# A hybrid encoder block's w_down products: where the fourth weight sum is made, and a place of its own for some raw weight blocks

## The chip, the cores and the metric

The kernel runs on one core of one Trainium2 chip. The metric is the time of one execution on the device in microseconds (us); the profile's page gives the span from the first to the last instruction of one execution. The engines are TensorE (PE: matmul; PEld: its weight loads), VectorE (DVE), ScalarE (ACT), GpSimd (POOL) and SyncE (SP), on which nearly all the transfers (DMA) of this kernel are issued. Each engine carries out its own instructions in order and waits for others through semaphores. SBUF is the on-chip memory in which tiles lie, PSUM the one that TensorE writes.

## The reference

One layer of an encoder on x of 1024 positions by 1024 channels, all in fp32:

```
h = RMSNorm(x)*(1+scale1)+shift1
[qA|kA|vA|qB|kB|vB|gA|gB] = h @ w_in
A: dilated sliding-window attention;  B: 2-D neighbourhood attention
m = sigmoid(gA)*(oA @ w_branch_dil) + sigmoid(gB)*(oB @ w_branch_na);  x += gate1 * (m @ w_out)
h2 = RMSNorm(x)*(1+scale2)+shift2;  u = depthwise_conv3(h2 @ w_up)
x += gate2 * ((gelu(u_g)*u_v) @ w_down)
y = RMSNorm_final(x)
```

The last product but the norm is the one that matters here: the GELU product a has 2816 channels (22 blocks of 128, called k-tiles), and w_down is 2816 by 1024.

## The kernel before, in words

**fp32 out of parts.** Each fp32 operand is split in two: a rounded copy, "hi", made by ScalarE, and the remainder, "lo" (source minus hi), made by GpSimd or VectorE (`split`, lines 57 and 61). A product takes three matmuls: hi·hi (line 1305), hi·lo (1306) and lo·hi (1307).

**Seven products for eight.** The large products are made in 2 × 2 blocks by a scheme of the Strassen-Winograd kind, with seven block products in place of eight. The weight blocks a11, a12, a21, a22 give seven left operands, in the order `11, S2, S1, S3, 12, S4, 22`, with

S1 = a21 + a22, S2 = S1 − a11, S3 = a11 − a21, S4 = a12 − S2.

`a_operands` makes them as a generator in four steps that the caller spreads over the products of the job before. It gets two raw blocks: raw[0] holds a11 and a12, raw[1] holds a21 and a22. GpSimd makes S1, S2 (both into one tile `ws` of the pool `big`) and S3 (in place of a21; lines 1255 to 1257). Then come the pairs: `whi`/`wlo` of raw[0], `wsh`/`wsl` of S2 and S1, `wsh`/`wsl` of S3 and a22. The fourth sum, S4, is VectorE's (line 1272), into a12's place in raw[0]; its hi and lo go into one more tile of `big`. So GpSimd has ten operations a job: three sums and seven remainders (128 × 384 each).

**The jobs of w_down.** Twelve jobs, numbered 0 to 11 (three groups of three pairs of k-tiles, times four pairs of row blocks q = 0 to 3), each of 7 × 3 × 3 = 63 matmuls of 128 × 512. While job n is multiplied, job n+1's weights are loaded (`down_load`, line 1419: two loads of 128 × 2 × 384, into two buffers `wraw`) and prepared. The pools set the rest: `whi`, `wlo`, `wsh`, `wsl` have two buffers or two and one, `big` nine, and PSUM six banks `pj`. `b_operands` loads and splits the right operands of the next group: six loads of 512 KB (line 1368), six GpSimd sums (1379, 1380) and splits (1359 to 1361). Results are put together by VectorE (1313 to 1330) and added to x (1411).

**What sets the order.** A list scheduler orders each engine's instructions after a simulated timeline. Two stretches are in the order of the code: SyncE's during jobs 0 to 2, and ScalarE's from the last w_up tile to job 2. A pool's buffer is used again when its last reader is done; the instruction that writes it waits for that.

**Names.** `pj` is a PSUM bank, `op` and `xb` are right operands, `x2` rows of x read back, `as` the GELU products in the chip's memory, `wc` a VectorE scratch tile. The number behind a name in the order is that of the instance.

Of the kernel before, what the change touches and what calls it, by code (L numbers as in the profile page):

```python
# [10 lines left out]
FT = mybir.dt.float32  # L11
FR = mybir.dt.float32r
AF = mybir.ActivationFunctionType
OP = mybir.AluOpType
# [5 lines left out]
KT = 8  # L20
# [4 lines left out]
G = 3  # L25
# [4 lines left out]
def hybrid_encoder(tc, xT, c, w_ada, small, w_in, p1_bias, p23_bias, na_bias, ln2_mult, ident, w_br, w_out,  # L30
                   w_up, w_down, out):
    nc = tc.nc
    act, dve, pool, pe, sp = nc.scalar, nc.vector, nc.gpsimd, nc.tensor, nc.sync

    const = tc.alloc_tile_pool(name="const", bufs=1)
    wpool = tc.alloc_tile_pool(name="w", bufs=2)
# [18 lines left out]
    def split(raw, hi, lo, lo_eng):  # L55

        act.activation(hi, raw, AF.Copy)  # L57
        n, cols = raw.shape[1], math.prod(raw.shape[1:])
        step = n // 2 if lo_eng is pool and cols > 512 and n % 2 == 0 else n
        for i in range(0, n, step):  # L60
            lo_eng.tensor_tensor(lo[:, i:i + step], raw[:, i:i + step], f(hi)[:, i:i + step], OP.subtract)  # L61
# [59 lines left out]
    work = tc.alloc_tile_pool(name="start", bufs=2, side="right", reuse_waits="tile")  # L121
# [150 lines left out]
    def v_wide(*sts):  # L272
        ps = [ps_s.tile([128, 512], FT, name="pv", bufs=3) if len(sts) == 1 else ps_g.tile([128, 512], FT, name="pj")
              for _ in sts]
        for k in range(KT):
            whi, wlo = (t[:, :, k] for t in v_all)
            for st, p in zip(sts, ps):
                hhi, hlo = (t[:, st % 4 * 128:st % 4 * 128 + 128] for t in h[st // 4, k])
                pe.matmul(p, hhi, whi, start=k == 0, stop=False)
                pe.matmul(p, hhi, wlo, start=False, stop=False)  # L280
                pe.matmul(p, hlo, whi, start=False, stop=k == KT - 1)
        return ps
# [136 lines left out]
    with tc.manual_schedule(engines={e.engine for e in (sp, act, dve, pool, pe)}):  # L419
# [37 lines left out]
        r = wpool.tile([128, KT], FT, name="rs", bufs=2)[:, :4]  # L457
# [18 lines left out]
        for q in range(4):  # L476
# [14 lines left out]
            last = 6 if q else 5  # L491
# [86 lines left out]
        for n, step in enumerate(v_steps[:9]):  # L578
# [14 lines left out]
            else:  # L593
                p = v_wide(*step[1:])
# [494 lines left out]
    for s in range(100):  # L1089
        n = 4 if s < 64 else 8 if s < 72 else 6 if s < 88 else 4  # L1090
# [24 lines left out]
    work = tc.alloc_tile_pool(name="gate", bufs=1, reuse_waits="tile")  # L1115
    o.append([work.tile([128, 4, S], FR, name=f"o1{n}") for n in ("hi", "lo")])
    g2 = g_scr.rearrange("(b m) p s -> m p b s", b=2)
    gates, ws, w_raw = {}, {}, {}
# [80 lines left out]
    for i in range(2 * KT):  # L1199
        m, hf = divmod(i, 2)  # L1200
# [16 lines left out]
        p = []  # L1217
# [22 lines left out]
    STEPS = (("11", "B11"), ("S2", "T2"), ("S1", "T1"), ("S3", "T3"), ("12", "B21"), ("S4", "B22"), ("22", "T4"))  # L1240
    names = tuple(b for _, b in STEPS)

    def a_operands(raw, n, work, st, lo_eng=pool, last=False, w_at=0, spot=None):


        spot = spot or big
        a11, a12, a21, a22 = raw[0][:, 0], raw[0][:, 1], raw[1][:, 0], raw[1][:, 1]
        ws = spot([128, 2, n, 128])
        S2, S1 = ws[:, 0], ws[:, 1]

        def pair(src, names, hi, lo, eng=pool):
            split(src, hi, lo, eng)
            for i, name in enumerate(names):
                st[name] = (hi[:, i], lo[:, i])
        pool.tensor_tensor(S1, a21, a22, OP.add)
        pool.tensor_tensor(S2, S1, a11, OP.subtract)
        pool.tensor_tensor(a21, a11, a21, OP.subtract)

        def outer(at):
            if w_at == at:  # L1260
                hi, lo = (wpool.tile([128, KT, 128], FR, name=t).rearrange("p (a b) m -> p a b m", a=2)[:, :, :n]
                          for t in ("whi", "wlo"))
                pair(raw[0], ("11", "12"), hi, lo, lo_eng)

        def s_tiles():
            pools = [work(t) for t in ("wsh", "wsl")]
            return [p.tile([128, 2, 4, 128], FR, name=t, bufs=b)[:, :, :n] for (p, b), t in zip(pools, ("wsh", "wsl"))]
        outer(0)
        yield
        pair(ws, ("S2", "S1"), *s_tiles())  # L1270
        if w_at != 3:
            dve.tensor_tensor(a12, a12, S2, OP.subtract)
        yield
        pair(raw[1], ("S3", "22"), *s_tiles())
        yield
        outer(3)
        if w_at == 3:
            dve.tensor_tensor(a12, a12, S2, OP.subtract)
        if last:
            p, b = work("wsl")  # L1280
            s4 = p.tile([128, 2, 4, 128], FR, name="wsl", bufs=b)[:, :, :n]
        else:
            s4 = spot([128, 2, n, 128], FR)
        pair(raw[0][:, 1:2], ("S4",), s4[:, 0:1], s4[:, 1:2])
        yield

    def products(st, n, moving, done, seq=range(7), in_psum=False, hold=None, spare=None):
# [46 lines left out]
    def reserve(tile_pool, tags):  # L1334
        for name, size, bufs in tags:
            tile_pool.tile([128, size // 4], FT, name=name, bufs=bufs)
# [7 lines left out]
    def big(shape, dtype=FT):  # L1344
        return keep.tile(shape, dtype, name="big", bufs=9)
# [63 lines left out]
    def acc(m, hf, src):  # L1409
        xx = x3[m, hf]  # L1410
        dve.scalar_tensor_tensor(xx, src, ada[:, 40 + m:41 + m], xx, OP.mult, OP.add)

    jobs = [(g0, q) for g0 in range(0, 9, G) for q in range(4)]

    def down_load(g0, q):
        raw = []
        for i in range(2):
            r = wpool.tile([128, KT, 128], FT, name="wraw").rearrange("p (a b) m -> p a b m", a=2)[:, :, :G]
            sp.dma_start(r, w_down[q + 4 * i].rearrange("p (a b) m -> p a b m", a=2)[:, :, g0:g0 + G])
            raw.append(r)  # L1420
        return raw
# [40 lines left out]
    def up_load(t):  # L1462
        raw = []
        for i in range(2):
            r = big([128, KT, 128]) if t in (0,) or t > 1 and t % 2 else wpool.tile([128, KT, 128], FT, name="wraw")
            sp.dma_start(r, w_up[t + FF * i])
            raw.append(r.rearrange("p (a b) m -> p a b m", a=2))
        return raw

    raw = [big([128, 2, 512]) for _ in range(4)]  # L1470
# [24 lines left out]
    raw = {0: up_load(0)}  # L1495
# [27 lines left out]

    work = tc.alloc_tile_pool(name="up", bufs=2, reuse_waits="tile")
    up2.append(work)
    tail, act_order, down_sts = [], contextlib.ExitStack(), [{} for _ in jobs]

    def extra(shape, dtype=FT):
# [53 lines left out]

    raw[1] = up_load(1)
    prep.append(a_operands(raw.pop(1), 4, s_home, sts[1], dve, spot=extra))
    next(prep[1])
    next(prep[1])
# [92 lines left out]
    nxt = a_operands(raw.pop(2), 4, s_home, sts[2], w_at=None, spot=extra)  # L1679
# [7 lines left out]
    for t in range(2, FF):  # L1687
        nxt = iter(())
        if t + 2 < FF:
            raw[t + 2] = up_load(t + 2)  # L1690
        if 0 < t < FF - 1:
            nxt = a_operands(raw.pop(t + 1), 4, s_home, sts[t + 1], last=t + 2 == FF)
            next(nxt)
        if t == FF - 1:
            act_order.enter_context(tc.manual_schedule(engines={act.engine}))
            next(first)
        for c, j in enumerate(gens[t] if t < 3 else up_products(t, sts[t])):
            if j in (1, 2, 5):
                next(nxt, None)
            if t == FF - 2 and j == 2:  # L1700
                more = b_operands(0, movs[0])
                next(more)
            if t == FF - 2 and j == 6:
                first = a_operands(down_load(*jobs[0]), G, s_home, down_sts[0])
                next(first)
                next(more)
            if t == FF - 1 and c in (1, 2, 5, 7, 9, 10, 13, 14, 16, 19, 20, 21, 23, 25, 26):
                next(more)
            if t == FF - 1 and c in (12, 17):
                next(first)  # L1710
# [3 lines left out]
    def x3_load(q):  # L1714
        for m, hf in ((q + 4, 1), (q, 0), (q, 1), (q + 4, 0)):
            x3[m, hf] = load_x(x_scr, hf, m)
# [4 lines left out]
    for n, (g0, q) in enumerate(jobs):  # L1721
        nxt = iter(())
        if n + 1 < len(jobs):
            nxt = a_operands(down_load(*jobs[n + 1]), G, s_home, down_sts[n + 1])
        if n < 3:
            x3_load(n + 1)
        if n == 2:
            sp_order.close()
            act_order.close()
        if q == 1:  # L1730
            more = b_operands(g0 + G, movs[g0 + G]) if g0 + G < 9 else end_operands(ends)
        for c, j in enumerate(products(down_sts[n], G, lambda b, k: movs[g0][b][k],
                                       lambda i, hf, src: acc(q + 4 * i, hf, src), in_psum=True)):
            if j in ((2, 3, 4, 5) if q == 0 else (0, 1, 2, 5)):
                next(nxt, None)
            if tail and (n, j) in ((0, 4), (0, 5), (1, 2), (2, 0)):
                tail.pop(0)()
            if (q == 1 and j in (2, 5) or q == 2 and j in (4, 5) or q == 3 and c in (1, 4, 5, 7, 9, 10, 12, 14, 15, 17, 18, 20)
                    or q == 0 and c in (1, 2, 4, 5, 7, 9, 10)):
                next(more, None)  # L1740
# [16 lines left out]
    with tc.manual_schedule(engines={dve.engine}):  # L1757
        for hf, cs in ((0, slice(0, 512)), (1, slice(0, 256)), (1, slice(256, 512))):
            n = cs.stop - cs.start
            late = []  # L1760
            for m in range(KT):
                if hf == 0 and m + 2 < KT:
                    end_w[m + 2] = end_weights(m + 2)
                p = ps.tile([128, 512], FT, name="pj", bufs=6)[:, :n]
# [140 lines left out]
```

## Time and profile before

| What | us |
| --- | --- |
| median of 3 runs | 1506.31 |
| lowest, highest | 1505.19, 1511.78 |
| profiled execution, its own time | 1512.37 |
| its span | 1510.6 |
| PE busy | 1483.4 (98% of the span) |
| DVE, ACT, POOL busy | 936.3, 772.9, 757.1 |
| mean granted TensorE clock | 0.992 |

The profiled execution is one of the long ones, 6.06 us above the median. A row of a view by stretches gives the stretch, its length, the busy time of each engine with the number of its instructions, the granted clock of TensorE (1.00 is full speed) and the share of the DMA engines' time. Rows of waits read "engine, what it made, line <- engine, what it waited for, line: total us, times, longest". A row of a timeline is: start, length, engine, line, operation, output<-inputs with shape, and in brackets the idle time just before, and for what.

### The profile page before, as it was taken

Reading aid. Unit: us, or ns where it says so; the run is one execution under the profiler, and the core shown is the slowest. Engines: PE = TensorE matmul, PEld = TensorE weight load, DVE = VectorE, ACT = ScalarE, POOL = GpSimd, SP = SyncE. Lnnn points to the kernel's source line nnn. Section 1 sums busy time; section 2 is a strip of 40 time slices with the busy share of each in tenths; the row PEclk is TensorE's granted clock in tenths of the full one; section 3 lists DMA queues with packets and bytes.
Section 4 is the critical chain, followed back from the end, with each engine's and each line's share of the span. In section 5 each row is a group of like instructions: output and inputs, shape, how many; then the busy total and the mean of one; then the engine's idle time right before and its main releaser. Section 6 shows DMA issues by size and latency. Waiting matters only on the chain.

```text
span 1510.6 us, 21652 instructions
## 1 busy us (share of the span) xinstructions
PE 1483.4 (98%) x7664; PEld 1259.5 (83%) x7664; DVE 936.3 (62%) x1763; ACT 772.9 (51%) x1442; POOL 757.1 (50%) x633
## 2 busy tenths in 40 slices
PE   9999999999999999999999999999999999999997
PEld 8887888889798998888888778888888888777887
DVE  6684446464545665566515897666666668786765
ACT  4531666666655566653345464444444448465442
POOL 2221333433234454512268678766666676777621
PEclk8999999999999999999999999999999999999999
DMA  9477333434745555577644213222222232631323
GB/s 371 178 258 255 90 108 77 146 92 133 181 131 152 142 164 165 172 246 252 198 157 142 93 46 137 84 84 84 84 84 84 85 133 91 210 130 49 114 57 112
DMA packets 117300, 210.28 MB, mean 139 GB/s; under 512 B 42788, under 2 KB 55716, under 8 KB 117156
## 3 DMA queue, kind: packets, MB, share of 16 engines
q1 hardware_dynamic: 116632, 208.57, 43.2%
q8 instruction: 60, 0.98, 0.3%
q14 instruction: 48, 0.39, 0.1%
q10 hardware_dynamic: 560, 0.33, 0.1%
HBM read 163.58 MB, written 42.66 MB: 137 GB/s over the span
## 4 chain that ended last, share of the span: by engine, by line
PE 77%; DMA 7%; DVE 6%; POOL 4%; ACT 2%; issue 2%; SPq 0%; DVEq 0%; POOLq 0%; ACTq 0%
PE pj L1307 10%; PE pj L1306 10%; PE pj L1305 10%; PE pj L84 10%; PE pj L86 10%; PE pj L85 10%; PE pj L402 3%; PE O L1013 2%; POOL wsl L61 1%; DMA wraw<-w_down 1%; PE T L1000 1%; DMA fb<-fcs 1%; PE S L978 1%; PE O L844 1%; DMA big<-as 1%
## 5 line engine op out<-in xcount | busy, mean ns | idle before, releaser
L61 POOL TENSOR_TENSOR wlo<-wraw,whi 128x512 fp32r<-128x512 f32 (+1 forms) x96 | 118.0, 1251 | 167.6 <-ACT whi L57 152.7
L84 PE MATMUL pj<-h,whi 128*128 128x512 f32 x432 | 178.2, 413 | 0.4 <-DVE kl L374 0.4
L86 PE MATMUL pj<-h,wlo 128*128 128x512 f32 x432 | 169.8, 393 | 0.0
L85 PE MATMUL pj<-h,whi 128*128 128x512 f32 x432 | 169.4, 392 | 0.0
L1305 PE MATMUL pj<-op,wsh 128*128 128x512 f32 x408 | 159.3, 390 | 1.1 <-ACT op L1236 0.6
L1306 PE MATMUL pj<-op,wsh 128*128 128x512 f32 x408 | 158.8, 390 | 0.9 <-DVE op L1237 0.6
L1307 PE MATMUL pj<-op,wsl 128*128 128x512 f32 x408 | 158.1, 390 | 0.7 <-POOL wsl L61 0.7
L667 DVE TENSOR_TENSOR tl<-T,th 128x512 fp32r<-128x512 f32 (+3 forms) x120 | 77.1, 654 | 102.0 <-ACT th L666 100.9
L717 POOL TENSOR_TENSOR wlo<-wraw,whi 128x512 fp32r<-128x512 f32 x58 | 74.2, 1290 | 126.2 <-ACT whi L716 126.1
L61 POOL TENSOR_TENSOR wsl<-big,wsh 128x512 fp32r<-128x512 f32 (+1 forms) x86 | 113.3, 1339 | 45.2 <-ACT wsh L57 39.7
L659 ACT ACTIVATE P<-P,st 128x256 f32<-128x256 f32 x128 | 64.2, 502 | 94.2 <-DVE st L658 94.2
L1538 DVE SCALAR_TENSOR_TENSOR big<-pj,sm,big 128x512 f32<-128x512 f32 (+2 forms) x183 | 94.9, 563 | 16.5 <-ACT big L1532 15.5
L86 PEld LDWEIGHTS pj<-h,wlo 128*128 128x128 f32 x432 | 81.1, 188 | 18.1
L1305 PE MATMUL pj<-op,whi 128*128 128x512 f32 x232 | 91.3, 393 | 3.1 <-ACT whi L57 3.1
L57 ACT ACTIVATE whi<-wraw 128x1024 fp32r<-128x1024 f32 (+2 forms) x51 | 49.5, 972 | 84.2 <-DMA wraw<-w_down 32.2
L1307 PE MATMUL pj<-op,wlo 128*128 128x512 f32 x232 | 91.2, 393 | 1.3 <-POOL wlo L61 1.3
L1305 PEld LDWEIGHTS pj<-op,wsh 128*128 128x128 f32 x408 | 76.6, 188 | 18.7 <-ACT wsh L57 1.5
L1307 PEld LDWEIGHTS pj<-op,wsl 128*128 128x128 f32 x408 | 76.6, 188 | 17.9 <-POOL wsl L61 2.2
L1306 PEld LDWEIGHTS pj<-op,wsh 128*128 128x128 f32 x408 | 76.6, 188 | 17.7 <-DVE op L1237 1.3
L84 PEld LDWEIGHTS pj<-h,whi 128*128 128x128 f32 x432 | 81.5, 189 | 11.5 <-issue 0.8
L1306 PE MATMUL pj<-op,whi 128*128 128x512 f32 x232 | 90.6, 391 | 0.0
L85 PEld LDWEIGHTS pj<-h,whi 128*128 128x128 f32 x432 | 81.7, 189 | 10.1
(392 smaller groups left out, 4176.2 us busy)
## 6 DMA issues: line engine op xcount, KB each, us to landing
wraw<-w_in SPq DMA_DIRECT2D x32, 512.0 KB
wada<-w_ada SPq DMA_DIRECT2D x31, 512.0 KB
big<-w_up SPq DMA_DIRECT2D x22, 512.0 KB
wraw<-w_up SPq DMA_DIRECT2D x22, 512.0 KB
big<-as SPq DMA_DIRECT2D x22, 512.0 KB
as<-big SPq DMA_DIRECT2D x21, 512.0 KB
wraw<-w_down SPq DMA_DIRECT2D x24, 384.0 KB
gs<-gs SPq DMA_DIRECT2D x32, 256.0 KB
```

The source lines that it names most:

```text
L57: act.activation(hi, raw, AF.Copy)
L61: lo_eng.tensor_tensor(lo[:, i:i + step], raw[:, i:i + step], f(hi)[:, i:i + step], OP.subtract)
L84: pe.matmul(psum, whi[:, k0 + k], mhi, start=k == 0, stop=False)
L85: pe.matmul(psum, whi[:, k0 + k], mlo, start=False, stop=False)
L86: pe.matmul(psum, wlo[:, k0 + k], mhi, start=False, stop=k == n - 1)
L659: act.activation(pp, pp, AF.Exp, bias=mi, scale=-1.0, accum_out=li)
L667: dve.tensor_tensor(tl[:m, :n], pt[:m, :n], f(th)[:m, :n], OP.subtract)
L717: pool.tensor_tensor(lo[:, i:i + n], raw[:, i:i + n], f(hi)[:, i:i + n], OP.subtract)
L1305: pe.matmul(psum, whi[:, k], bhi, start=j < 4 and k == 0, stop=False, skip_group_check=True)
L1306: pe.matmul(psum, whi[:, k], blo, start=False, stop=False, skip_group_check=True)
L1307: pe.matmul(psum, wlo[:, k], bhi, start=False, stop=k == n - 1, skip_group_check=True)
L1538: dve.scalar_tensor_tensor(y[:, dst], src, wt, y[:, dst], OP.mult, OP.add)
```

## The change

`a_operands` gets an argument `apart`. Where it is set, as in all twelve jobs of w_down and in none of w_up, S4 is written where S1 was, `ws[:, 1]`, and its hi and lo are made from there. The raw block is only read. And for odd q, so in jobs 1, 3, 5, 7, 9 and 11, the first raw block goes into a tile `xr` of its own (128 × 2 × 3 × 128 fp32, 3072 bytes a partition) in the pool `work`, in place of one of the two `wraw` buffers; `reserve` keeps room for it. Line numbers behind it grow by one to five.

```diff
-    def a_operands(raw, n, work, st, lo_eng=pool, last=False, w_at=0, spot=None):
+    def a_operands(raw, n, work, st, lo_eng=pool, last=False, w_at=0, spot=None, apart=False):
...
         pair(ws, ("S2", "S1"), *s_tiles())
+        S4 = S1 if apart else a12
         if w_at != 3:
-            dve.tensor_tensor(a12, a12, S2, OP.subtract)
+            dve.tensor_tensor(S4, a12, S2, OP.subtract)
...
-        pair(raw[0][:, 1:2], ("S4",), s4[:, 0:1], s4[:, 1:2])
+        pair((ws if apart else raw[0])[:, 1:2], ("S4",), s4[:, 0:1], s4[:, 1:2])
...
         for i in range(2):
-            r = wpool.tile([128, KT, 128], FT, name="wraw").rearrange("p (a b) m -> p a b m", a=2)[:, :, :G]
+            if i == 0 and q % 2:
+                r = work.tile([128, 2, G, 128], FT, name="xr", bufs=1)
+            else:
+                r = wpool.tile([128, KT, 128], FT, name="wraw").rearrange("p (a b) m -> p a b m", a=2)[:, :, :G]
...
     up2.append(work)
+    reserve(work, (("xb", 4096, 2), ("wsh", 4096, 1), ("wsl", 4096, 1), ("xr", 3072, 1)))
...
-                first = a_operands(down_load(*jobs[0]), G, s_home, down_sts[0])
+                first = a_operands(down_load(*jobs[0]), G, s_home, down_sts[0], apart=True)
...
-            nxt = a_operands(down_load(*jobs[n + 1]), G, s_home, down_sts[n + 1])
+            nxt = a_operands(down_load(*jobs[n + 1]), G, s_home, down_sts[n + 1], apart=True)
```

The scheduler moves instructions with it. On SyncE, from the last of the six loads of right operands to the loads of jobs 3 to 6, before (wraw_12265 and 12267 are job 3's raw blocks, 12392 and 12394 job 4's, 12563 and 12565 job 5's, 12705 and 12707 job 6's):

```order
L1368 DMA big_12207<-as_7878 128x1024
L1577 DMA as_7878<-big_12085 128x1024
L1419 DMA wraw_12265<-w_down 128x2x384
L1419 DMA wraw_12267<-w_down 128x2x384
L1171 DMA x2_12269<-xs_7877 128x512
...
L1419 DMA wraw_12392<-w_down 128x2x384
L1419 DMA wraw_12394<-w_down 128x2x384
L1419 DMA wraw_12563<-w_down 128x2x384
L1419 DMA wraw_12565<-w_down 128x2x384
L1419 DMA wraw_12705<-w_down 128x2x384
L1419 DMA wraw_12707<-w_down 128x2x384
```

and in the changed kernel at the same place (12269 and 12271 are job 3's, 12396 and 12398 job 4's, 12567 and 12569 job 5's, 12709 and 12711 job 6's, xr_12836 is job 7's first):

```order
L1423 DMA xr_12269<-w_down 128x2x384
L1423 DMA wraw_12271<-w_down 128x2x384
L1171 DMA x2_12273<-xs_7877 128x512
...
L1582 DMA as_7878<-big_12089 128x1024
L1423 DMA wraw_12396<-w_down 128x2x384
L1423 DMA xr_12567<-w_down 128x2x384
L1423 DMA wraw_12398<-w_down 128x2x384
L1423 DMA wraw_12569<-w_down 128x2x384
L1423 DMA wraw_12709<-w_down 128x2x384
L1423 DMA xr_12836<-w_down 128x2x384
L1423 DMA wraw_12711<-w_down 128x2x384
```

The store of a GELU product moved behind job 3's loads and those of x, and the first block of each odd job moved ahead of the second block of the even job before it.

On GpSimd, the work for jobs 3 and 4 before:

```order
L61 TENSOR_TENSOR wlo_12296<-wraw_12265,whi_12295 128x384 x2
L1255 TENSOR_TENSOR big_12291<-wraw_12267 128x384
L1256 TENSOR_TENSOR big_12291<-big_12291,wraw_12265 128x384
L1257 TENSOR_TENSOR wraw_12267<-wraw_12265,wraw_12267 128x384
L61 TENSOR_TENSOR wsl_12313<-big_12291,wsh_12312 128x384 x2
L61 TENSOR_TENSOR wsl_12331<-wraw_12267,wsh_12330 128x384 x2
L61 TENSOR_TENSOR big_12373<-wraw_12265,big_12373 128x384
L1255 TENSOR_TENSOR big_12413<-wraw_12394 128x384
L61 TENSOR_TENSOR wlo_12418<-wraw_12392,whi_12417 128x384 x2
```

and in the changed kernel:

```order
L61 TENSOR_TENSOR wlo_12300<-xr_12269,whi_12299 128x384 x2
L1255 TENSOR_TENSOR big_12295<-wraw_12271 128x384
L1256 TENSOR_TENSOR big_12295<-big_12295,xr_12269 128x384
L1257 TENSOR_TENSOR wraw_12271<-xr_12269,wraw_12271 128x384
L61 TENSOR_TENSOR wlo_12422<-wraw_12396,whi_12421 128x384 x2
L61 TENSOR_TENSOR wsl_12317<-big_12295,wsh_12316 128x384 x2
L61 TENSOR_TENSOR wsl_12335<-wraw_12271,wsh_12334 128x384 x2
L61 TENSOR_TENSOR big_12377<-big_12295,big_12377 128x384
L1255 TENSOR_TENSOR big_12417<-wraw_12398 128x384
```

Job 4's two remainders of the raw block (wlo_12422) moved ahead of job 3's four wsl remainders, and S4's remainder (big_12377) now reads the tile `ws`.

On VectorE, around job 3's S4 sum, before:

```order
L1411 SCALAR_TENSOR_TENSOR x2_12134<-pj_12279,ada_70,x2_12134 128x512
L1326 TENSOR_TENSOR pj_12318<-pj_12318,wc_12289 128x512
L1272 TENSOR_TENSOR wraw_12265<-wraw_12265,big_12291 128x384
L1411 SCALAR_TENSOR_TENSOR x2_12136<-pj_12318,ada_70,x2_12136 128x512
L1330 TENSOR_TENSOR pj_12335<-pj_12335,wc_12289 128x512
L1411 SCALAR_TENSOR_TENSOR x2_12138<-pj_12335,ada_70,x2_12138 128x512
```

and in the changed kernel:

```order
L1412 SCALAR_TENSOR_TENSOR x2_12138<-pj_12283,ada_70,x2_12138 128x512
L1327 TENSOR_TENSOR pj_12322<-pj_12322,wc_12293 128x512
L1412 SCALAR_TENSOR_TENSOR x2_12140<-pj_12322,ada_70,x2_12140 128x512
L1362 TENSOR_TENSOR op_12407<-stage_12408,op_12407 128x512
L1331 TENSOR_TENSOR pj_12339<-pj_12339,wc_12293 128x512
L1412 SCALAR_TENSOR_TENSOR x2_12142<-pj_12339,ada_70,x2_12142 128x512
L1273 TENSOR_TENSOR big_12295<-xr_12269,big_12295 128x384
```

The sum moved four instructions back, behind the results that are put together and added to x.

More of the change, by code (lines that the diff above doesn't have):

```diff
@@ L1277, in a_operands @@
         if w_at == 3:
-            dve.tensor_tensor(a12, a12, S2, OP.subtract)
+            dve.tensor_tensor(S4, a12, S2, OP.subtract)
         if last:
```

## The prediction

> **What bounds the kernel now.** I read the page of the whole execution first, then the trace cut into stretches, then TensorE's waits, then the chain of work that ended last, and last the timeline of one stall.
>
> ```profile
> span 1510.6 us, 21652 instructions
> PE 1483.4 (98%) x7664; PEld 1259.5 (83%) x7664; DVE 936.3 (62%) x1763; ACT 772.9 (51%) x1442; POOL 757.1 (50%) x633
> ```
>
> TensorE is busy in 98% of the span. The change adds and removes no matmul, so the most it can win is TensorE's lost time in the stage that it touches. The built programs agree in order up to the fourth weight sum of w_down's first job, about 1251 us in. The stretches (time, then busy time and count of PE, PEld, DVE, ACT, POOL, then granted clock, DMA share, GB/s) tell where time is lost behind that:
>
> ```profile
> 1262.00:1297.00 35.00, 35.00 (x156) 28.96 (x155) 29.19 (x46) 21.52 (x38) 21.39 (x22) 1.00 0.58 194
> 1297.00:1394.00 97.00, 89.80 (x371) 70.37 (x370) 68.36 (x99) 57.25 (x99) 77.85 (x75) 0.96 0.33 110
> 1394.00:1441.00 47.00, 47.00 (x209) 38.90 (x208) 33.52 (x50) 22.14 (x38) 31.83 (x32) 1.00 0.32 103
> ```
>
> TensorE is full before 1297 and after 1394 us. Between them it is idle for 97.0 − 89.8 = 7.2 us, and its pace is lower too. With TensorE alone, over a longer full stretch:
>
> ```profile
> 1228.00:1297.00 69.00, 69.00 (x306) 1.00 0.44 148
> ```
>
> The undisturbed pace is 69.0/306 = 0.2255 us per matmul, so a job of 63 matmuls takes 14.2 us. The 371 matmuls recorded between 1297 and 1394 need 83.7 us, with a few missing records (up to 375) 84.6. So 97.0 − 84.6 = 12.4 us are lost there. Busy time shows less than that, since a matmul that waits, or runs at the lower clock, still counts as busy. What TensorE waits for in the down stage (total, times, longest):
>
> ```profile
> PE pj L1305 <- ACT whi L57: 4.7, 4, 1.7
> PE pj L1307 <- POOL wlo L61: 1.3, 1, 1.3
> PE pj L1307 <- POOL wsl L61: 0.7, 1, 0.7
> PE pj L1305 <- ACT wsh L57: 0.4, 1, 0.4
> ```
>
> All of it is weight preparation, made while the job before is multiplied. What ScalarE, GpSimd and the load queue wait for between 1260 and 1440 us shows what holds the preparation:
>
> ```profile
> POOL wlo L61 <- ACT whi L57: 21.5, 6, 4.5
> POOL big L1255 <- DMA wraw<-w_down: 14.0, 3, 5.6
> ```
>
> ```profile
> ACT whi L57 <- DMA wraw<-w_down: 32.2, 9, 5.8
> ```
>
> ```profile
> SPq L1419 <- POOL wsl L61: 31.6, 11, 5.2
> SPq L1419 <- POOL big L61: 25.2, 10, 11.5
> ```
>
> ScalarE and GpSimd wait for the load of raw weights, and the load waits for GpSimd's last readings of the raw blocks of the job before. That is a loop. One turn of it on GpSimd (the last column in brackets is the idle time before, and for what):
>
> ```profile
> 1318.20 1.03 POOL L61 TENSOR_TENSOR big<-wraw,big 128x384 fp32r<-128x384 f32 x1
> 1323.89 1.02 POOL L1255 TENSOR_TENSOR big<-wraw 128x384 f32<-128x384 f32 x1 [4.67 <-DMA wraw<-w_down]
> 1324.86 2.01 POOL L61 TENSOR_TENSOR wlo<-wraw,whi 128x384 fp32r<-128x384 f32 x2
> 1326.82 1.03 POOL L1256 TENSOR_TENSOR big<-big,wraw 128x384 f32<-128x384 f32 x1
> 1327.80 1.02 POOL L1257 TENSOR_TENSOR wraw<-wraw 128x384 f32<-128x384 f32 x1
> 1329.11 2.01 POOL L61 TENSOR_TENSOR wsl<-big,wsh 128x384 fp32r<-128x384 f32 x2 [0.29 <-ACT wsh L57]
> 1331.07 2.00 POOL L61 TENSOR_TENSOR wsl<-wraw,wsh 128x384 fp32r<-128x384 f32 x2
> 1333.02 1.02 POOL L61 TENSOR_TENSOR big<-wraw,big 128x384 fp32r<-128x384 f32 x1
> ```
>
> From one S4 remainder to the next 14.82 us pass, of which 4.67 us GpSimd sits idle until the load is there. TensorE needs only 14.2. Loads differ, by the chain (start, length):
>
> ```profile
> 1319.25 4.51 DMA wraw<-w_down
> ...
> 1333.09 3.51 DMA wraw<-w_down
> ...
> 1379.99 5.42 DMA wraw<-w_down
> ```
>
> Ten readings and sums of about 1.02 us plus a load of 3.5 to 5.4 give 13.7 to 15.6 us a turn. The worst stall is the end of such a turn:
>
> ```profile
> 1384.59 0.84 ACT L57 ACTIVATE whi<-wraw 128x768 fp32r<-128x768 f32 x1 [3.75 <-DMA wraw<-w_down]
> ...
> 1385.48 0.50 PE L1305 MATMUL pj<-op,whi 128*128 128x512 f32 x1 [1.70 <-ACT whi L57]
> ...
> 1387.56 0.80 PE L1307 MATMUL pj<-op,wlo 128*128 128x512 f32 x1 [1.35 <-POOL wlo L61]
> ```
>
> ```profile
> 1386.50:1393.20 6.70, 5.64 (x13) 0.50 0.00 0
> ```
>
> The last row is the stretch right behind it, TensorE alone: the granted clock is 0.50. Its 13 matmuls would take 2.9 us at full pace.
>
> **The change part by part.** *S4 goes into S1's place.* No instruction is added. VectorE's sum (1.35 us) reads the same inputs and writes elsewhere. Two things follow. The raw block is given back when the sum has been made, and not after S4's remainder on GpSimd, which is the tenth of ten operations. And the sum must wait until GpSimd has read S1, that is for the seventh operation: in the turn above it could begin at 1331.1 in place of 1327.9, 3.2 us later. The order moves it four instructions back on VectorE (by some 0.7 us each, the length of its rows below), so I cost that wait at nothing; at worst VectorE stands 3.2 us, the full move, in each of 8 jobs.
>
> *A home for the first raw block of odd jobs.* No instruction is added here either, and 3 KB per partition are free at that place. The first block's load, of odd and even jobs alike, no longer waits for the end of the job before; it waits for readings about one job earlier. So the hi copy and the two wlo remainders, which TensorE waited for five times, leave the loop.
>
> *The loop that is left* is that of the second block. Its place is free after nine of ten operations (9 × 1.02 = 9.2 us), or after the seventh and VectorE's sum (7 × 1.02 + 1.35 = 8.5 us). With the load: 12.0 to 14.6 us. Against 14.2 on TensorE only the longest loads still lose, 0.4 us a job.
>
> *GpSimd's six sums for the next operands* (lines 1379 and 1380), once in four jobs, stand in the same queue. Their row is here, with the issues of the loads, VectorE's S4 sums and one of VectorE's ordinary rows (least, median and greatest duration in ns, then first and last start):
>
> ```profile
> L1379 POOL TENSOR_TENSOR wc<-big x6: 1277/1290/1294, 1295.7 to 1367.2; 128x512 f32<-128x512 f32 x6
> ```
>
> ```profile
> L1419 SPq DMA_DIRECT2D wraw<-w_down x24: 539/545/637, 1222.1 to 1426.1; - x24
> ...
> L1272 DVE TENSOR_TENSOR wraw<-wraw,big x12: 548/1352/1364, 1251.5 to 1432.9; 128x384 f32<-128x384 f32 x12
> ```
>
> ```profile
> 1318.42 0.69 DVE L1361 TENSOR_TENSOR op<-stage,op 128x512 fp32r<-128x512 f32 x1 [1.34 <-ACT op L1360]
> ```
>
> They are 6 × 1.29 = 7.7 us per four jobs. GpSimd's work is then 10.2 + 7.7/4 = 12.1 us a job, under 14.2: it isn't the bound if it needn't sit idle for loads. The order now puts the next job's two wlo ahead of job 3's four wsl, so that a late load of job 4 holds job 3's remainders as well. By TensorE's order in the built program, the hi tile's buffer is given up some 35 matmuls (7.9 us) ahead of use, against 0.84 + 2 × 1.02 = 2.9 us of work, which leaves 5.0. I cost it at 0, and at 2.0 (both remainders late) at the most.
>
> *The load queue.* As many loads are issued (24, 0.55 us each). The store of a GELU product goes behind two loads of w_down and four of x, which costs nothing, since it is read only in the last third of the jobs; at most one issue, 0.55 us. A load of job 7 is now queued ahead of job 6's second one and the six loads of the next operands: its wait holds those. The nearest price is the 0.4 us above in the good case and the 4.67 us of idle GpSimd in the bad one.
>
> *Sum.* Lost before: 12.4 us. Left: 0.4 us in four to eight jobs, 1.6 to 3.2, middle 2.4. So −10.0 us: 1512.4 of the profiled execution (span 1510.6 and 1.8 around it) becomes 1502.4. That execution is 6.1 us above the median of 1506.31. One part of it that differs easily lies at its start, which the change doesn't touch:
>
> ```profile
> 14.00:28.00 14.00, 14.00 (x63) 13.42 (x62) 7.99 (x15) 5.72 (x9) 3.46 (x3) 0.51 1.02 391
> ```
>
> Half a clock for 14 us costs up to 7 us. If the 6.1 us lie there, the median becomes 1506.3 − 10.0 = 1496.3; I take 1496. If they lie in the stalls between 1297 and 1394, the median run loses only about 6.3 there and would end near 1502.
>
> [...]
>
> **The rivals.**
> (A) Nearly all waits go: 1493 to 1498.5, as worked out. Against it speaks only what the trace of before can't show, how the new order behaves.
> [...]
> (C) About half of the waits stay, because GpSimd's burst of 7.7 us comes whole between two jobs' remainders, or the queue's new order holds the six operand loads: −5, about 1501. For it: stalls stand close behind the first burst (the sums begin at 1295.7, the first stalls in the cut from 1297). Against it: with the home, the hi copy no longer waits behind the burst.
> (D) Nothing measurable: the loop only moves to the second block, whose 14.6 us plus the burst's 1.9 a job are no shorter than before; 1504 to 1508.
> (E) Slower: the sum on VectorE stands until GpSimd has read S1, and VectorE's evictions of TensorE's results stand behind it in order. The price is 3.2 us a job, and four neighbours at 0.69 us cover 2.8. If the cover is gone in eight jobs, 8 × 3.2 = 25.6 against the 12.4 won: +13, about 1519. It decides once the stand costs TensorE over 12.4/8 = 1.6 us a job. Against it: VectorE is 68.36 of 97 us busy there, and TensorE has not waited once for VectorE in this stage.
>
> **How the numbers follow.** Chances: A 0.57, B 0.14, C 0.13, D 0.06, E 0.10. A change of 0.5%, 7.5 us, is about what a measurement of this kernel can tell from none: faster means under 1498.8, slower over 1513.8. Nearly all of A (0.54), a third of B (0.05) and a fifth of C (0.03) are faster: 0.62. E gives 0.10 slower, and 0.28 lie between. The low end is A with nothing left and a little less loss at the half clock, 1506.3 − 12.4 − 2 = 1492. The high end takes in B, C and the start of D: 1504.5.
>
> **What would show it.** Between 1297 and 1394 us, stretches of that length in which TensorE holds 0.226 us a matmul, with clock 1.00 throughout. No wait of line 1306 for the hi copy over 0.5 us. GpSimd's remainder of S4 again about 14.2 us after the last. The loads of odd jobs' first block landing one job before use. VectorE's fourth sum three microseconds later after line 1256 than before. Wrong I would be if TensorE waited for VectorE, if GpSimd still sat 4 us idle for a load in each job with the hi copy behind it, or if time were lost ahead of 1251 us, where nothing has changed.

## The result and the profile after

The changed kernel takes 1498.67 us in the median of 5 runs (1496.19 to 1500.06), against 1506.31. The ratio is 0.9943, with a 95% interval from 0.9927 to 0.9958. That is 7.6 us or 0.51% less, 0.1 us beyond the 0.5% that was called faster: on which side of that line it falls is chance, since the runs spread over 3.9 us. Five more runs on another chip gave 1499.01 us, ratio 0.9940 (0.9926 to 0.9955). The forecast was 1496.0 in a range from 1492.0 to 1504.5.

The profiled execution took 1498.67 us with a span of 1496.8. It is 13.8 us shorter in span than the one before, nearly twice the gain of the medians. The stretches (PE, PEld, DVE, ACT, POOL, then clock, DMA share, GB/s) show a first piece of it, at the start, in which the two programs are the same:

```profile
14.00:28.00 14.00, 13.33 (x101) 11.93 (x100) 11.39 (x19) 5.73 (x9) 7.55 (x7) 1.00 1.03 397
...
1297.00:1394.00 97.00, 93.18 (x402) 74.42 (x402) 73.38 (x106) 60.00 (x105) 79.31 (x77) 1.00 0.31 99
```

In 14 to 28 us TensorE issued 101 matmuls at clock 1.00, where the profile before has 63 at 0.51. How much that is can be read at GpSimd's first sum of w_down, ahead of the first place where the programs differ. Before and after, by the rows of the tile `wraw` (least/median/greatest ns, then first and last start):

```profile
L1255 POOL TENSOR_TENSOR big<-wraw x12: 1003/1015/1029, 1244.0 to 1430.7; 128x384 f32<-128x384 f32 x12
```

```profile
L1255 POOL TENSOR_TENSOR big<-wraw x12: 1006/1016/1062, 1237.6 to 1410.3; 128x384 f32<-128x384 f32 x12
```

The profile after was 6.4 us ahead there by chance, and 5.3 us of it by 56 us already (the remainder `vwl` on GpSimd starts at 50.39 in place of 55.73). The rest is 13.8 − 6.4 = 7.4 us, and that agrees with the medians.

In the stage of w_down the clock stayed at 1.00, and TensorE's waits between 1230 us and the end of the jobs are these:

```profile
PE pj L1306 <- ACT wsh L57: 2.7, 3, 1.5
PE pj L1308 <- POOL wsl L61: 0.7, 2, 0.4
PE pj L1306 <- DVE pj L1319: 0.3, 1, 0.3
```

The waits for the hi copy `whi` (4.7 us before) and for `wlo` (1.3) are gone. The waits that are left are for weights made from S1 to S3. Added up gap by gap between matmuls, TensorE lost 11.4 us before and 5.0 after between 1240 and 1441 us. By the pace, as the prediction counts it between 1297 and 1394, it is 12.4 before and 97.0 − 402 × 0.2255 = 6.3 after.

By the rows, what is left hangs on a wait that the change itself made. In VectorE's, the load queue's and GpSimd's waits of the changed kernel, 1255 to 1430 us:

```profile
DVE big L1273 <- POOL wsl L61: 13.4, 6, 4.4
```

```profile
SPq L1423 <- DVE big L1273: 67.7, 8, 15.4
```

```profile
POOL big L1255 <- DMA wraw<-w_down: 16.5, 9, 4.4
```

S4's sum waits for GpSimd to finish reading S1; the load waits for the sum, since the raw block is free only then; and GpSimd waits for the load, once nearly every job. The longest of TensorE's waits shows this chain row by row, on GpSimd, VectorE, the load queue, ScalarE and TensorE:

```profile
1346.04 2.55 POOL L1380 TENSOR_TENSOR wc<-big 128x512 f32<-128x512 f32 x2
1348.56 1.29 POOL L1381 TENSOR_TENSOR big<-big,wc 128x512 f32<-128x512 f32 x1
1349.81 1.29 POOL L1380 TENSOR_TENSOR wc<-big 128x512 f32<-128x512 f32 x1
1351.06 1.27 POOL L1381 TENSOR_TENSOR big<-big,wc 128x512 f32<-128x512 f32 x1
1352.30 1.97 POOL L61 TENSOR_TENSOR wsl<-big,wsh 128x384 fp32r<-128x384 f32 x2
1354.25 1.99 POOL L61 TENSOR_TENSOR wsl<-wraw,wsh 128x384 fp32r<-128x384 f32 x2
1356.20 1.29 POOL L1381 TENSOR_TENSOR big<-big,wc 128x512 f32<-128x512 f32 x1
...
1361.63 1.02 POOL L1255 TENSOR_TENSOR big<-wraw 128x384 f32<-128x384 f32 x1 [2.07 <-DMA wraw<-w_down]
1362.73 1.00 POOL L1256 TENSOR_TENSOR big<-big,xr 128x384 f32<-128x384 f32 x1
```

```profile
1354.31 3.60 DVE L1273 TENSOR_TENSOR big<-wraw,big 128x384 f32<-128x384 f32 x1 [4.07 <-POOL wsl L61]
```

```profile
1357.93 1.22 SPq L1423 DMA_DIRECT2D wraw<-w_down  x2
```

```profile
1363.76 0.84 ACT L57 ACTIVATE wsh<-big 128x768 fp32r<-128x768 f32 x1 [5.29 <-POOL big L1256]
```

```profile
1364.66 0.50 PE L1306 MATMUL pj<-op,wsh 128*128 128x512 f32 x1 [1.51 <-ACT wsh L57]
```

The rows show one thing more. Five of GpSimd's six sums (lines 1380 and 1381) ran from 1346.04 to 1352.33, just ahead of the remainder `wsl` that VectorE's sum waited for, and the sixth ran while that sum was made. By the rows, both hold this stall up, the new wait and the burst.

### The profile page after: what moved, and what is told of

Read it like the earlier page. It is cut to its first block, busy times and chain, and to the rows that moved or that the text cites. A ratio compares the mean times of both kernels' runs of the same rounds, so it can differ in the third digit from the quotient of the medians.

```text
span 1496.8 us, 21659 instructions
## 1 busy us (share of the span) xinstructions
PE 1474.4 (98%) x7664; PEld 1251.9 (84%) x7664; DVE 939.0 (63%) x1763; ACT 773.6 (52%) x1442; POOL 760.6 (51%) x633
## 4 chain that ended last, share of the span: by engine, by line
PE 81%; DVE 5%; POOL 5%; DMA 4%; issue 2%; ACT 2%; SPq 0%; DVEq 0%; POOLq 0%; ACTq 0%
PE pj L84 10%; PE pj L86 10%; PE pj L85 10%; PE pj L1308 10%; PE pj L1307 10%; PE pj L1306 10%; PE pj L402 3%; PE O L1013 2%; DMA wraw<-w_down 2%; PE T L1000 1%; PE S L978 1%; POOL wsl L61 1%; PE pv L279 1%; PE pv L281 1%; PE pv L280 1%
## 5 line engine op out<-in xcount | busy, mean ns | idle before, releaser
L61 POOL TENSOR_TENSOR wlo<-wraw,whi 128x512 fp32r<-128x512 f32 (+1 forms) x84 | 106.1, 1284 | 144.8 <-ACT whi L57 129.8
L61 POOL TENSOR_TENSOR wsl<-wraw,wsh 128x384 fp32r<-128x384 f32 (+1 forms) x46 | 57.3, 1268 | 62.1 <-ACT wsh L57 54.5
```

## The experiments

Three questions were open. Which of the two parts wins the 7.6 us? Is the 5.0 us that is left due to S4's wait, to the number or the sharing of the places, or to GpSimd's six sums? And is there a better kernel? Each diff is against the changed kernel. The ratios are to the kernel before on the same chip, with 95% intervals. Each edit also lets the scheduler set another order; no run changes a place and keeps the order.

**The parts alone.** First S4's new place without the home:

```diff
-            if i == 0 and q % 2:
+            if False:
...
-    reserve(work, (("xb", 4096, 2), ("wsh", 4096, 1), ("wsl", 4096, 1), ("xr", 3072, 1)))
```

> S4 goes into S1's place, and all raw blocks stay in the two wraw buffers. The loop theory: a block is given back after nine GpSimd operations or after VectorE's sum, and not after ten, so a turn is shorter by 1.0 to 1.7 us, 12.0 to 14.6 in place of 13.7 to 15.6, but the hi copy stays in it. About half of the 7.6 us that the change won: 3 to 5 us, 1501 to 1503. The rival that the home does it all: 1505 to 1507, and TensorE's waits for the hi copy as long as before (4.7 us). The rival that S4's place does it all: 1498 to 1500.

Measured: 1505.73 us, ratio 0.9994 (0.9981 to 1.0007). By itself this part wins nothing that can be told from noise (the interval allows 2.9 us at most), and the loop theory's 3 to 5 us did not come. The waits of TensorE didn't go; they changed places. None is for the hi copy, though that is still in the loop (three rows of its waits):

```profile
PE pj L1308 <- POOL wlo L61: 2.4, 1, 2.4
PE pj L1306 <- ACT wsh L57: 1.6, 2, 0.9
PE pj L1306 <- ACT wc L1312: 1.4, 1, 1.4
```

VectorE's sum waited for GpSimd's remainders in that kernel too:

```profile
DVE big L1273 <- POOL wsl L61: 13.2, 7, 4.5
```

Then the home without S4's new place:

```diff
-                first = a_operands(down_load(*jobs[0]), G, s_home, down_sts[0], apart=True)
+                first = a_operands(down_load(*jobs[0]), G, s_home, down_sts[0], apart=False)
...
-            nxt = a_operands(down_load(*jobs[n + 1]), G, s_home, down_sts[n + 1], apart=True)
+            nxt = a_operands(down_load(*jobs[n + 1]), G, s_home, down_sts[n + 1], apart=False)
```

> The first raw block of odd jobs has its home, and S4 is made in the raw block as before. The loop theory: the hi copy leaves the loop (its 4.7 us of TensorE's waits go), but the second block's load waits for the tenth GpSimd operation of a job: 3 to 5 us of the 7.6 won, 1501 to 1503, with waits for the wsh copies in place of the whi copies. The rival that the home does it all: 1498 to 1500. The rival that S4's place does it all: 1505 to 1507.

Measured: 1497.65 us, ratio 0.9930 (0.9913 to 0.9947), the whole gain of the change. So the rival that the home does it all has both times about right, but not its sign in the run before: there TensorE's 4.7 us for the hi copy were to stay, and they went. TensorE waits for no weights at all in its profile:

```profile
PE pj L1306 <- ACT op L1361: 1.5, 1, 1.5
PE pj L1306 <- DVE pj L1319: 0.2, 1, 0.2
```

**How the three places are shared.** Every third raw block goes into the home:

```diff
+    blocks = itertools.count()
...
-            if i == 0 and q % 2:
+            if next(blocks) % 3 == 2:
```

> The changed kernel, but each third raw block in turn goes into the home, so that the three places are used in rotation and every load waits for the block three before it; in the changed kernel an even job's second block waits for the block two before. If the leftover of 5.0 us comes from how the three places are shared out: 2 to 4 us faster than the changed kernel, 1494.5 to 1496.5. If it comes from S4's sum that waits for GpSimd: 1498 to 1499.5, since the second block then waits for the first block of the job before, which that sum still reads.

Measured: 1499.14 us, ratio 0.9937 (0.9918 to 0.9955), as the changed kernel. Its profile has one wait for weights left (wsh, 1.1 us). The median shows nothing of that; its profiled execution met the half clock at the start (64 matmuls at 0.51 in 14 to 28 us), as the profile before did. The same rotation with S4 in the raw block (both edits together):

> S4 is made in the raw block as before the change, and each third raw block in turn goes into the home. If S4's place doesn't matter once there is a third place (as the run with the home alone has it): 0.992 to 0.995, like the changed kernel. If the rotation makes the second block's load wait for the tenth operation on the first block of the job before, and that counts: 0.996 to 0.999.

Measured: 1497.87 us, ratio 0.9942 (0.9930 to 0.9955). With a third place, neither the choice between S1's place and the raw block nor the sharing shows in the time; the second outcome named there did not come.

**GpSimd's six sums.** They are left out for the groups behind the first, whose operands T1 to T3 are then made from the unsummed blocks, so that this kernel doesn't compute the layer. That frees 7.7 us of GpSimd twice:

```diff
-        t1 = [wide() for _ in range(G)]
-        for k in range(G):
+        t1 = [wide() for _ in range(G)] if g0 == 0 else [x[1] for x in b]
+        for k in range(G if g0 == 0 else 0):
```

> The changed kernel without GpSimd's six sums for the next right operands in the groups behind the first (they are left out, and the operands T1, T2 and T3 of those groups are made from the unsummed blocks). If GpSimd's burst of 7.7 us causes what TensorE still loses (5.0 us between 1297 and 1394): 3 to 5 us faster than the changed kernel, 0.990 to 0.992 of the kernel before, and at most 1.5 us of waits left. If the places of the raw blocks or S4's sum cause it: 0 to 1 us, 0.993 to 0.995, with waits for the wsh copies as now.

Measured: 1497.54 us, ratio 0.9938 (0.9925 to 0.9951). By the ratios that is 0 to 1 us better than the change (0.9943 and 0.9940), which can't be told from none. Yet the waits for wsh went from its profile too; it has two others, of 1.0 and 0.6 us, for VectorE. The two signs don't agree, and the run doesn't settle it. The same sums on VectorE:

```diff
-            pool.tensor_tensor(t1[k], t2, b11, OP.subtract)
-            pool.tensor_tensor(t2, b22, t1[k], OP.subtract)
+            (dve if g0 else pool).tensor_tensor(t1[k], t2, b11, OP.subtract)
+            (dve if g0 else pool).tensor_tensor(t2, b22, t1[k], OP.subtract)
```

> The changed kernel with these six sums made by VectorE (six times about 0.7 us) in place of GpSimd. If the burst on GpSimd costs TensorE and VectorE has room (it is busy 73 of 97 us there): 2 to 5 us faster than the changed kernel, 0.990 to 0.993. If VectorE's evictions come late by it: TensorE waits for VectorE's results in its banks, and the time is that of the changed kernel or up to 4 us more, 0.994 to 0.997.

Measured: 1496.66 us, ratio 0.9939 (0.9924 to 0.9953). TensorE waits for no weights there either, only 0.6 us for VectorE. Against the changed kernel the gain isn't distinct. So the waits for wsh also go from the profile when the burst leaves GpSimd, as the rows of the longest one suggest; what that is worth in time, these two runs don't resolve.

**S4 in a tile of its own.** First in one of the five scratch tiles:

```diff
-        S4 = S1 if apart else a12
+        S4 = wide()[:, :128 * n].rearrange("p (n m) -> p n m", m=128) if apart else a12
...
-        pair((ws if apart else raw[0])[:, 1:2], ("S4",), s4[:, 0:1], s4[:, 1:2])
+        pair((S4.rearrange("p (o n) m -> p o n m", o=1) if apart else raw[0][:, 1:2]), ("S4",), s4[:, 0:1], s4[:, 1:2])
```

> The changed kernel, but S4 is made in a scratch tile of its own (one of the five wc tiles) and not in S1's place, so that VectorE's sum needs not wait until GpSimd has read S1, and the raw block is given back some 3 us earlier. If that new wait causes what TensorE still loses between 1297 and 1394 us (5.0 us, mostly waits for the wsh copies): 2 to 4 us faster than the changed kernel, 1494.5 to 1496.5, and VectorE's waits for GpSimd's wsl (13.4 us) gone. If the leftover comes from the number of places or from long loads: 1498 to 1499.5. If the scratch tiles are short: slower than 1500.

Measured: 1503.79 us, ratio 0.9972 (0.9957 to 0.9986), slower than the change. VectorE's wait for wsl was gone, as expected, but another order came with it: GpSimd works without a pause from 1295 to 1316 us and is late, TensorE waits 2.0 us for wsh and 2.1 for wsl, and eight matmuls behind that run at half the clock:

```profile
1311.61 0.50 PE L1306 MATMUL pj<-op,wsh 128*128 128x512 f32 x1 [2.00 <-ACT wsh L57]
1314.89 0.79 PE L1308 MATMUL pj<-op,wsl 128*128 128x512 f32 x1 [2.09 <-POOL wsl L61]
```

```profile
1315.00:1318.20 3.20, 3.20 (x8) 0.52 0.03 12
```

Then in one of the nine big tiles, so that the scratch tiles are left to the six sums:

```diff
-        S4 = S1 if apart else a12
+        S4 = spot([128, n, 128]) if apart else a12
```

(The second line of the edit, that of `pair`, is as above.)

> As the run with S4 in a scratch tile, but in a tile of the nine big ones. It tells whether that run's loss came from the five scratch tiles, which the six sums also use. If so: as the changed kernel or 1 to 3 us faster, 0.992 to 0.994. If an earlier S4 sum doesn't help, since GpSimd's order is what is late there: 0.996 to 0.998 again.

Measured: 1496.01 us, ratio 0.9929 (0.9916 to 0.9942), the first of the outcomes. So it wasn't the earlier sum that cost that time, but the scratch tile with the order that came with it; these two the runs don't separate. The last four runs put this beside the changed kernel on one chip:

> The changed kernel beside the three others of this call, on the same chip: 0.993 to 0.9955 of the kernel before.

> The changed kernel with S4 in a big tile of its own. If the wait of S4's sum for GpSimd's reading of S1 is what is left of TensorE's lost time: 2 to 4 us faster than the changed kernel of this call. If not: within 1 us of it.

> S4 in a big tile of its own and the six sums on VectorE. If each of the two already takes nearly all of TensorE's lost time in the stage (0.9 and 0.8 us left in their profiles): no faster than either alone, 0.9915 to 0.9935. If their waits are different ones that hide each other: 1 to 2 us faster than either.

> No home for raw blocks, and S4 in a big tile of its own, so that neither the raw block nor S1 is held. The run with S4 in S1's place and no home won nothing. If that was because the sum had to wait for GpSimd to read S1 (13.2 us of VectorE's waits in that run): 3 to 6 us faster than before, 0.996 to 0.998. If with two places the second block's remainders, operations eight and nine, hold the load whatever S4 does: 0.998 to 1.0005.

| Kernel | median us | ratio to before | interval |
| --- | --- | --- | --- |
| the change | 1499.01 | 0.9940 | 0.9926 to 0.9955 |
| S4 in a big tile, with the home | 1495.75 | 0.9924 | 0.9906 to 0.9943 |
| the same, and the six sums on VectorE | 1500.03 | 0.9955 | 0.9934 to 0.9976 |
| S4 in a big tile, no home | 1495.09 | 0.9923 | 0.9902 to 0.9944 |

With the home, S4 in a big tile is 3.3 us faster by the medians than S4 in S1's place, as expected if that wait is what is left; the earlier runs gave 0.9929 against 0.9943. Each time the intervals overlap. In its profile TensorE's lost time in the stage is 0.9 us (3.3 for the changed kernel on that chip), with one wait over 0.3:

```profile
PE pj L1306 <- DVE pj L1319: 0.4, 1, 0.4
```

The last row of the table is the one that tells most. There is no home, only two places, and it is as fast as any: a single other tile for S4, in place of S1's, with the order that goes with it, turns 0.9994 into 0.9923, and both intervals are far apart. VectorE's sum no longer waits for wsl; what is left of its waits for GpSimd is

```profile
DVE big L1273 <- POOL big L1256: 4.7, 2, 3.4
```

So two places would have done, and with S4 in S1's place this part took back nearly all that it gave. With both cures together nothing more is won, since TensorE is full. With the sums on VectorE as well, TensorE waits for VectorE instead, and the median is 4.3 us higher. The intervals just overlap, so that the loss isn't certain (its profiled execution, 1507.00 us, also met the half clock at the start, 63 matmuls at 0.51):

```profile
PE pj L1306 <- DVE x L1412: 2.3, 2, 1.9
```

## Why the prediction was right, and where not

*The bound.* Right: the lost time between 1297 and 1394 us was the loop of raw blocks, and it went in large part. With the waits went the half clock behind the worst stall: the mean clock of this stretch is 0.96 before and 1.00 after. Two kernels that cure the loop in different ways, the home alone and the big tile without a home, agree on that (1.00 in both). The prediction shows two rows of the load queue's waits; the longest, between 1260 and 1440 us, it leaves out:

```profile
SPq L1419 <- ACT wsh L57: 52.8, 7, 12.0
```

Its reading holds all the same. ScalarE's copy `wsh` and GpSimd's remainder `wsl` read the same block, and `wsl` comes later. Before the turn that it shows, the queue waits 5.7 us for the copy, which ends at 1314.89, and then 3.3 us for the remainder, which ends at 1318.24; the load is issued at 1318.27.

*The sum.* The step that was mis-sized is "Left: 0.4 us in four to eight jobs, 1.6 to 3.2, middle 2.4". Measured were 5.0 us in one profile of the change and 3.3 in the other. The gain of the medians is 7.6 us on the first chip and 8.5 on the second, in place of 10.0: 2.4 and 1.5 short, of which this term, 2.6 and 0.9 too small, is the most by either profile. The pace named as a sign, 0.226 us a matmul, wasn't reached either: 97.0/402 = 0.241.

*Why it was too small.* The prediction costed the wait of S4's sum "at nothing", because the order moves the sum four instructions back on VectorE. It asked only whether VectorE would stand, and named TensorE's results as what would be late. VectorE did stand, 13.4 us in six waits, but it had the time. Late were the raw block that the sum gives back, and so the next load. The first consequence named there, that the block is given back earlier, was counted as a gain, and the second, the wait, as free; the run of this part alone shows that the two nearly cancel (0.9994, 0.9981 to 1.0007). The loop of 8.5 us to the sum's end also took 1.35 us for the sum; it was 3.60 in the stall above. And the burst stood in that stall ahead of the sum; the prediction costs it at 0, with 2.0 at the most.

*The home.* Right, and more than that: alone it is worth the whole. Its reason, that the hi copy leaves the loop, agrees with the waits (4.7 us to none) but isn't shown by them, since they also went in the run without the home. Nor is the home the only cure, as the run with S4 in a big tile and no home shows.

*The profiled execution.* "If the 6.1 us lie there", at the start, was the right choice: 6.4 us lay ahead of w_down, 5.3 of them in the first 56 us.

*The clock.* The high end of the range, and 0.14 of the chances, take in B, an ordinary run of before that loses less to the half clock behind the worst stall than the profiled one. That is the author's estimate: no run shows how often the drop comes there. What the runs showed is the mean clock. On the chip of the last runs, that of twelve runs of before is 0.9931, of five of the change 0.9964. In the clock records of the two profiles, before and after, it is 1.00 or 0.50. If it is so in all runs, (1 − clock) times the span is the most that the half clock can have cost: 10.4 and 5.4 us. Of either, some 2 to 3.5 us are the end of the kernel, at 0.50 with TensorE all but done (4.6 us in the profile before, 6.9 in the one after). So by this estimate some 5 us of the gain there (8.5 us by the medians) can be clock and not waits. Some of that is the start, which differs by chance (63 matmuls before and 101 after in the same 14 us), and some the half clock behind stalls (6.8 us of it between 1297 and 1394 us in the profile before, none in the one after). How much of each can't be told from the means.

*The rivals.* The time, 1498.67, lies 0.2 us above (A)'s range and 2.3 below (C)'s 1501. (C), the burst or the queue: of TensorE's listed waits 3.7 of 7.1 us stayed, about the half that (C) names, and the burst stands in the longest; but leaving the six sums out won only 0 to 1 us by the ratios. (D) is excluded by the interval. (E): TensorE waited 0.3 us for VectorE, against the 1.6 a job from which it would decide.

## What to carry to other kernels

When a value is moved out of a buffer to give that buffer back sooner, look at who still reads the place it moves to: here that reader was the engine that the buffer had been waiting for, and one more tile was worth as much as a third place for raw blocks. Cost a new wait by what the waiting instruction releases, not only by what stands behind it on its engine. Where a profiled execution lies some us off the median, look for a stretch of half clock before counting its stalls as gain.

## What the runs showed of the hardware

*VectorE's fourth sum took longer with GpSimd's operations beside it.* The same sum, 128 × 384, takes 0.55 us where GpSimd is idle beside it (1393.26 in the changed kernel; GpSimd is idle from 1393.03 to 1394.45). It takes 1.35, near the median, in the turn that the prediction shows: one GpSimd operation starts there at 1327.80 and ends at 1328.82, the sum starts at 1327.88 and ends 0.4 us after it. It took 3.60 where three GpSimd operations ran back to back beside it (the fence above: 1354.25 to 1357.49). Its least, median and greatest in the changed kernel, for the six jobs whose first block lies in `wraw`:

```profile
L1273 DVE TENSOR_TENSOR big<-wraw,big x6: 556/1356/3596, 1253.0 to 1408.1; 128x384 f32<-128x384 f32 x6
```

Both of the longer sums end 0.4 us after the last of the GpSimd operations beside them, near the 0.55 us that the sum takes alone, as if it had been made behind them. No run was made on it, so the cause isn't shown.

*The clock fell where TensorE was busy all the time by the profile.* In three of the fourteen profiles (the home alone, every third block, and S4 in a big tile without a home), the clock goes to half late in the kernel with no wait ahead of it. By the first, TensorE alone:

```profile
1458.50:1461.00 2.50, 2.50 (x25) 1.00 0.00 0
1461.00:1462.40 1.40, 1.40 (x15) 1.00 0.00 0
1462.40:1465.50 3.10, 3.10 (x17) 0.52 0.00 0
```

Among the matmuls ahead are column sums with one moving column (these 24 in the run with every third block):

```profile
L98 PE MATMUL pcol<-ones,wc x24: 168/250/250, 1461.0 to 1464.7; 128*128 128x1 f32 x24
```

The other profiles have these matmuls without a drop there (1.00 in every row of that stretch), and no run was made on it: what makes the clock fall stays open. By the rows, the half clock lasts about 3.4 us in each of the three.

*The start.* Programs that are identical there had 63 or 64 matmuls at clock 0.51 in 14 to 28 us in four of the fourteen profiles, and 93 to 102 at 0.93 to 1.00 in the ten others. By the clock record of the profile before, the half clock near the start lasts 13.7 us (14.4 to 28.0); at half speed that costs up to 6.8 us, nearly the gain of the change. The record after has none there. Behind the worst stall, by the same record of before, the half clock lasts 6.8 us.
